# A decoder trunk on one core: GpSimd multiplies the keys by their decays, VectorE the queries, and 64 stationary keys for blocks of 64

## The chip, the cores and the metric

The kernel runs on one core of a Trainium2 chip. A core has TensorE (PE in the rows; PEld is its weight load), VectorE (DVE), ScalarE (ACT), GpSimd (POOL) and SyncE (SP), which here issues the loads. The metric is the time of one execution on the device in microseconds, the median of several runs.

## What is computed

A trunk of two pre-norm layers over 256 tokens of width 2048: the first mixes tokens with HGRN2 (12 heads of 128), the second with gated linear attention (GLA, 4 heads with keys of 192 and values of 384). Both share a projection with a cross attention into 256 memory tokens, and each layer ends with a SwiGLU feed-forward. All is float32. What matters here is the recurrence of both mixers, cut from the reference:

```python
def _chunk_gated_linear_attention(q, k, v, log_a):
    """S_t = diag(exp(log_a_t)) S_{t-1} + k_t v_t^T ; o_t = S_t^T q_t, causal."""
    ...
        diff = cum[:, :, :, None, :] - cum[:, :, None, :, :]
        decay = jnp.exp(jnp.where(mask[:, :, None], diff, -jnp.inf))
        scores = jnp.einsum('bhtd,bhsd,bhtsd->bhts', qc, kc, decay)
        intra = jnp.einsum('bhts,bhse->bhte', scores, vc)
```

A score of query t with key s thus carries, in each channel, the product of all decays between s and t.

## The kernel before

Every large matmul multiplies in two parts: a weight tile arrives by DMA as `raw` (four blocks of 128x512), ScalarE casts it to a rounded part, VectorE subtracts that from the raw tile to get the rest, both into a `parts` tile, and TensorE makes three products of them with the two parts of the activations. `project_two` goes over eight pairs of row blocks; a pair of kind S takes seven products instead of eight, for which VectorE first forms sums and differences of the raw blocks. At the end VectorE and ScalarE add the products up. So ScalarE, VectorE and TensorE work in a chain on tile after tile, and TensorE takes its instructions strictly in the program's order.

The scores stand between these projections. HGRN has three groups of four heads (`hgrn_group`), GLA two pairs of two heads (`gla_pair`). `gated_scores` makes the scores of all 256 tokens by doubling: queries `Q` and keys `K` lie with the 128 channels on the partitions. Level by level, for blocks of m = 1, 2, 4, ... 64 tokens, TensorE multiplies each second block of queries with the keys, 128 tokens at a time (`score`; `sdh`, `sph`, `slh` and `pxh` in HGRN, `sdg`, `spg`, `slg` and `pxg` in GLA are its banks). VectorE then copies what belongs to the level from the bank to the scores `sc` under a mask (`place`, the COPY_PREDICATED rows), and `grow(m)` multiplies the queries of the odd blocks by the decay of the block's first part and the keys of the even blocks by the decay of the second, so that both are right for the next level. The decay products `T` of all levels are made beforehand by `decays`. After level 64 `across` multiplies the second half's queries with all keys of the first (`pxh`, `pxg`). At a level m the stationary operand is the first `keys` tokens of 128; `keys` was `max(P - m, 96)`: 124, 120, 112, 96, 96 for blocks of 4 to 64.

Each level is a piece in a list (`later`). `project_two` calls `step()` at set places, and so puts a piece between its products. The tile framework then orders the instructions of each engine by its own plan and places the semaphores. `pe`, `ve` and `ac` are wrappers, which is why nearly all rows carry their one line, L141; instructions that are given to `nc.gpsimd` directly carry their own. GpSimd does little before: memsets, and the power -1/2 of each root mean square (`rstd`, L179).

Of the kernel before, what the change touches and what calls it, by code (L numbers as in the profile page):

```python
# [14 lines left out]
ALU = mybir.AluOpType  # L15
AX = mybir.AxisListType

P = 128
# [5 lines left out]
MIX = 1536  # L24
# [4 lines left out]
DK = 192  # L29
DV = 384  # L30
# [5 lines left out]
def trunk_kernel(ctx: ExitStack, tc: tile.TileContext, x, mem, norm_mix, norm_ffn, norm_mem,  # L36
                 norm_final, hgrn_w_in, hgrn_lb_logits, hgrn_onorm, gla_w_in, gla_w_gk,
                 gla_b_gk, gla_onorm, w_mem_kv, w_out, w_gate_up, w_down, c_ident, c_mask, out):
    nc = tc.nc
# [112 lines left out]
    pe, ve, ac = Engine(nc.tensor), Engine(nc.vector), Engine(nc.scalar)  # L152
# [83 lines left out]
    def later(*pieces):  # L236
        pending.extend(pieces)
# [13 lines left out]
    def side(shape, name):  # L251
        return wts.tile(shape, F32, tag="parts", name=name, bufs=6)
# [400 lines left out]
    def new_ss(name):  # L653
        return small.tile([P, NT, NQ], F32, tag="hss", name=name)
# [60 lines left out]
    for l in range(2):  # L715
        kv = side([P, 2, XH * T], f"kv{l}")
# [5 lines left out]
        if l == 0:  # L722
# [4 lines left out]
            hq, ss, first_turns = {}, new_ss("ss_x"), []  # L727
# [103 lines left out]
    def gated_scores(st, heads, name):  # L831

        nh = len(heads)
        ng = NT * nh

        def place(at, cols, i, ps, m):

            rows, n = ps.shape[0], at.shape[1]
            nb = 64 // m
            ve.copy_predicated(
                out=at[0:rows].rearrange("p g (b o m) -> p g b o m", o=2, m=m)[:, :, :, cols, :],
                mask=mask[0:rows, i, :].rearrange("p (b m) -> p b m", m=m).unsqueeze(1).broadcast_to([rows, n, nb, m]),
                data=ps.rearrange("p g (b m) -> p g b m", m=m))

        def grow(m):

            Q, K = st["Q"], st["K"]  # L850
            nb = K.shape[1] * T // (2 * m)
            tv = st["T"][m].rearrange("p (b o) -> p b o", o=2)
            qv = Q[:, 0, :, :].rearrange("p n (b o m) -> p (n b) o m", o=2, m=m)[:, :, 1 if m > 1 else 0, :]
            kv = K.rearrange("p n (b o m) -> p (n b) o m", o=2, m=m)[:, :, 0, :]
            ve.tensor_tensor(out=qv, in0=qv, in1=tv[:, :, 0].unsqueeze(2).broadcast_to([P, nb, m]), op=ALU.mult)
            ve.tensor_tensor(out=kv, in0=kv, in1=tv[:, :, 1].unsqueeze(2).broadcast_to([P, nb, m]), op=ALU.mult)

        def score(ps, f, t, q, i, parts, n=P):
            pe.matmul(ps[0:n], st["K"][:, f, t * P:t * P + n], q, start=i == 0, stop=i == len(parts) - 1)

        def even_diagonal():
            sc = st["sc"] = work.tile([P, ng, P], F32, tag="sc", name=f"sc{name}")
            nc.gpsimd.memset(sc, 0.0)
            ps = aux_ps(f"sd{name}").rearrange("p (g c) -> p g c", c=64)
            for t in range(NT):
                for a, parts in enumerate(heads):
                    for i, f in enumerate(parts):
                        q = st["Q"][:, 0, f, t * P:(t + 1) * P].rearrange("p (c o) -> p c o", o=2)[:, :, 0]
                        score(ps[:, t * nh + a, :], f, t, q, i, parts)
            place(sc, 0, 0, ps[:, 0:ng, :], 1)  # L870
            grow(1)

        def pairs():
            sc = st["sc"]
            for t in range(NT):
                ps = aux_ps(f"sp{name}{t}").rearrange("p (g x c) -> p g x c", x=2, c=64)
                for a, parts in enumerate(heads):
                    for i, f in enumerate(parts):
                        q = st["Q"][:, :, f, t * P:(t + 1) * P].rearrange("p x (b o m) -> p x b o m", o=2, m=2)[:, :, :, 1, :]
                        score(ps[:, a, :, :].rearrange("p x (b m) -> p x b m", m=2), f, t, q, i, parts)  # L880
                place(sc[:, t * nh:(t + 1) * nh, :], 1, 1, ps[:, 0:nh, 1, :], 1)
                place(sc[:, t * nh:(t + 1) * nh, :], 1, 2, ps[:, 0:nh, 0, :], 2)
            grow(2)

        def level(li):
            m = LEVELS[li]

            keys = max(P - m, 96)
            ps = aux_ps(f"sl{name}{m}").rearrange("p (g c) -> p g c", c=64)
            for t in range(NT):  # L890
                for a, parts in enumerate(heads):
                    for i, f in enumerate(parts):
                        q = st["Q"][:, 0, f, t * P:(t + 1) * P].rearrange("p (b o m) -> p b o m", o=2, m=m)[:, :, 1, :]
                        score(ps[:, t * nh + a, :].rearrange("p (b m) -> p b m", m=m), f, t, q, i, parts, keys)
            place(st["sc"], 1, 1 + li, ps[0:keys, 0:ng, :], m)
            grow(m)

        def across():
            scx = st["scx"] = work.tile([P, nh, P], F32, tag="scx", name=f"scx{name}")
            px = aux_ps(f"px{name}")  # L900
            for a, parts in enumerate(heads):
                for i, f in enumerate(parts):
                    score(px[:, a * P:(a + 1) * P], f, 0, st["Q"][:, 0, f, P:T], i, parts)
            ac.copy(out=scx.rearrange("p a t -> p (a t)"), in_=px[:, 0:nh * P])

        return [even_diagonal, None, pairs, None, lambda: level(2), lambda: level(3), None, lambda: level(4),
                lambda: level(5), None, lambda: level(6), across]

    def readout(st, a, nh, t, v, ops):
# [78 lines left out]
    def gla_pair(w, pr, dec, decay, hq, r, yq):  # L988

        kw = MIX // 2  # L990
# [15 lines left out]
        def read(a):  # L1006
            hd = 2 * pr + a
            for t in range(NT):
                po = aux_ps(f"gpo{hd}{t}")
                readout(st, a, 2, t, lambda s: v[a][:, s, :], po[:, 0:DV])  # L1010
                ss = small.tile([P, 4], F32, tag="oss", name=f"goss{hd}{t}")
                square_sum(po[:, 0:DV], ss[:, 0:1], f"go{hd}{t}")
                ro = rstd(ss[:, 0:1], 1, DV, f"gro{hd}{t}")
                ve.scalar_tensor_tensor(out=gate[a][:, t, :], in0=po[:, 0:DV], scalar=ro[:, 0:1],
                                               in1=gate[a][:, t, :], op0=ALU.mult, op1=ALU.mult)

        def turn_y(a):
            hd = 2 * pr + a
            for i in range(3):
                f = 3 * hd + i  # L1020
                q, k = divmod(f, 4)
                if k == 0:
                    yq[q] = Quad("tq", f"y1_{q}")
                tp = transposes([lambda t: gate[a][:, t, i * P:(i + 1) * P]], f"ty1_{f}")
                yq[q].put(k, 1, tp[:, 0:T], g_go[:, i:i + 1])
# [3 lines left out]
        def give():  # L1029
            for name in "kq":  # L1030
                dst.append(work.tile([P, NT, 2, T], F32, tag="stg", name=f"gs{name}{pr}", bufs=2))
                nc.gpsimd.memset(dst[-1][:, :, :, DK:T], 0.0)
            return [lambda t, d=d: d[:, t, :, 0:DK] for d in dst]

        project_two(hq["pairs"], "------S-", w, kw + pr * 2 * DK, pr * 2 * DK, 2 * DK, f"gk{pr}", give,
                    lambda ps: ps.rearrange("p (a c) -> p a c", c=DK))
        for d in dst:
            for t in range(NT):
# [3 lines left out]
        if pr == 0:  # L1042
            scores[5:5] = [lambda: decay(1), None]
        later(None, None, turn_k, turn_q, None, *scores)
        gate, v = [], []
        for a in range(2):
            def give():
                for dst, tag in ((gate, "gate"), (v, "v")):
                    dst.append(work.tile([P, NT, DV], F32, tag=tag, name=f"g{tag}{pr}{a}"))
                return [lambda t, d=d[a]: d[:, t, :] for d in (gate, v)]  # L1050

            project_two(hq["pairs"], "-----SS-" if a == 0 else "-----SS-", w, 2 * kw + MIX + (2 * pr + a) * DV, 2 * kw + (2 * pr + a) * DV, DV,
                        f"gg{pr}{a}", give)
            for dst, func in ((gate[a], AF.Silu), (v[a], AF.Copy)):
                for t in range(NT):
                    ac.activation(out=dst[:, t, :], in_=dst[:, t, :], func=func, scale=r[:, t:t + 1])
            later(None, None, lambda a=a: read(a), None, lambda a=a: turn_y(a))

    def gla(hq, r, yq):
# [47 lines left out]
        for pr in range(2):  # L1107
            gla_pair(w, pr, dec, decay, hq, r, yq)
# [114 lines left out]
    for l in range(2):  # L1223
# [33 lines left out]
        if l == 0:  # L1257
            hq = {}
# [81 lines left out]
```

## Time and profile before

| | us |
|---|---|
| median of three runs | 2284.35 (2283.91 to 2284.79) |
| the profiled execution | 2283.64 |
| its span in the trace | 2281.9 |
| TensorE busy | 2267.8 (99%) |
| VectorE busy | 2086.5 (91%) |
| ScalarE busy | 1404.9 (62%) |
| GpSimd busy | 35.3 (2%) |

The granted clock of TensorE was 2.4 GHz throughout (0.999 of it over the span). The scores take five stretches of the span: 180 to 255, 285 to 360 and 386 to 447 us in HGRN, 1297 to 1350 and 1416 to 1465 in GLA. A busy TensorE in the page is one that has matmuls in flight; how many it finishes is read from the starts of neighbouring rows. A row's duration includes a tail that overlaps the next instruction, so that what an instruction costs its engine is the distance to the next start.

### The profile page before, as it was taken

How to read it: one execution, taken by the hardware profiler on the slowest of the kernel's cores; microseconds unless marked ns; L12 is line 12 of the kernel's file. 1: busy time of each engine (PE TensorE's matmuls, PEld its weight loads, DVE VectorE, ACT ScalarE, POOL GpSimd, SP SyncE). 2: the span in 40 equal slices, each digit the busy share in tenths (PEclk: the TensorE clock that was granted, in tenths of full speed). 3: DMA queues.
4: the chain of work that ended last, by engine and by line, in shares of the span. 5: the costliest groups of instructions: out<-in, count | busy, mean ns of one | idle time of the engine just before them, and what ended most of it. 6: DMA issues, size and time to landing. Idle time of an engine off the chain costs nothing.

```text
span 2281.9 us, 29717 instructions
## 1 busy us (share of the span) xinstructions
PE 2267.8 (99%) x10942; PEld 1922.5 (84%) x10942; DVE 2086.5 (91%) x2605; ACT 1404.9 (62%) x1918; POOL 35.3 (2%) x39
## 2 busy tenths in 40 slices
PE   9999999999999999999999999999999999999998
PEld 7888888888888888888889999988888888888887
DVE  7889999799999999999997887889999999999997
ACT  7655546466666666666665665466566666666664
POOL 0000000000000000000000000001000000000000
PEclk9999999999999999999999999999999999999999
DMA  8545545545556655565565446455565566556664
GB/s 292 198 161 167 185 148 184 166 150 202 184 203 206 213 191 202 200 206 203 201 209 179 140 143 190 144 184 203 180 208 203 203 200 206 203 201 205 204 210 158
DMA packets 231650, 435.57 MB, mean 191 GB/s; under 512 B 12204, under 2 KB 41680, under 8 KB 231248
## 3 DMA queue, kind: packets, MB, share of 16 engines
q1 hardware_dynamic: 230208, 429.41, 55.9%
q10 hardware_dynamic: 1296, 4.26, 0.5%
q8 instruction: 86, 1.41, 0.2%
q14 instruction: 60, 0.49, 0.1%
HBM read 430.48 MB, written 3.15 MB: 190 GB/s over the span
## 4 chain that ended last, share of the span: by engine, by line
PE 86%; issue 9%; DVE 3%; ACT 1%; DMA 0%; POOL 0%; SPq 0%; POOLq 0%; DVEq 0%; ACTq 0%
PE f_p L141 36%; PE fd L141 19%; PE wo L141 4%; PE hv2p L141 2%; PE m1p L141 2%; PE wo0p L141 2%; PE wo1p L141 2%; PE fd_0p L141 2%; PE m0p L141 2%; PE gk1p L141 1%; PE gg10p L141 1%; PE gg11p L141 1%; PE gg01p L141 1%; PE gx L141 1%; DVE raw L141 1%
## 5 line engine op out<-in xcount | busy, mean ns | idle before, releaser
L141 DVE TENSOR_TENSOR raw<-raw 128x512 f32<-128x512 f32 (+3 forms) x474 | 403.0, 851 | 9.4
L141 DVE TENSOR_TENSOR parts<-raw,parts 128x1024 fp32r<-128x1024 f32 (+1 forms) x216 | 246.3, 1179 | 15.5 <-ACT parts L141 15.5
L141 ACT CAST parts<-raw 128x1024 fp32r<-128x1024 f32 (+1 forms) x216 | 211.7, 1017 | 45.1 <-DMA raw<-in_w_out_dram 9.1
L141 ACT COPY h<-fd 128x512 f32<-128x512 f32 x80 | 46.0, 588 | 51.9 <-PE fd L141 49.2
L141 ACT ACTIVATE s<-s,rf_r 128x512 f32<-128x512 f32 x44 | 31.9, 725 | 44.5 <-DVE s L141 44.5
L141 DVE TENSOR_TENSOR e<-f_p,e 128x512 f32<-128x512 f32 x66 | 45.1, 684 | 2.7 <-DVE s L141 0.5
L141 ACT COPY fd<-h 128x512 f32<-128x512 f32 x82 | 45.2, 583 | 0.0
L141 PE MATMUL fd<-parts,s_2h 128*128 128x512 f32 x128 | 39.8, 392 | 0.0
L141 PE MATMUL fd<-parts,s_8h 128*128 128x512 f32 x128 | 39.8, 392 | 0.0
L141 PE MATMUL fd<-parts,s_4h 128*128 128x512 f32 x128 | 39.8, 392 | 0.0
L141 PE MATMUL fd<-parts,s_0h 128*128 128x512 f32 x128 | 39.8, 392 | 0.0
L141 PE MATMUL fd<-parts,s_6h 128*128 128x512 f32 x128 | 39.8, 392 | 0.0
L141 PE MATMUL fd<-parts,s_1h 128*128 128x512 f32 x128 | 39.4, 389 | 0.0
L141 PE MATMUL fd<-parts,s_7h 128*128 128x512 f32 x128 | 39.4, 389 | 0.0
L141 PE MATMUL fd<-parts,s_3h 128*128 128x512 f32 x128 | 39.4, 389 | 0.0
L141 PE MATMUL fd<-parts,s_5h 128*128 128x512 f32 x128 | 39.4, 389 | 0.0
L141 DVE TENSOR_TENSOR s<-f_p,e 128x512 f32<-128x512 f32 x44 | 30.3, 688 | 4.6 <-PE f_p L141 2.8
L141 DVE SCALAR_TENSOR_TENSOR s<-e,rf_r,s 128x512 f32<-128x512 f32 x44 | 31.0, 745 | 0.2
L141 PEld LDWEIGHTS fd<-parts,s_3h 128*128 128x128 f32 x128 | 24.0, 188 | 5.0
L141 PEld LDWEIGHTS fd<-parts,s_1h 128*128 128x128 f32 x128 | 24.0, 188 | 5.0
L141 PEld LDWEIGHTS fd<-parts,s_7h 128*128 128x128 f32 x128 | 24.0, 188 | 5.0
L141 PEld LDWEIGHTS fd<-parts,s_5h 128*128 128x128 f32 x128 | 24.0, 188 | 5.0
(5696 smaller groups left out, 7231.6 us busy)
## 6 DMA issues: line engine op xcount, KB each, us to landing
raw<-in_w_gate_up_dram SPq DMA_DIRECT2D x352, 512.0 KB, 4.1
raw<-in_w_down_dram SPq DMA_DIRECT2D x80, 1024.0 KB, 5.1
raw<-in_hgrn_w_in_dram SPq DMA_DIRECT2D x96, 512.0 KB, 4.0
raw<-in_gla_w_in_dram SPq DMA_DIRECT2D x96, 384.0 KB, 3.5
raw<-in_w_out_dram SPq DMA_DIRECT2D x16, 1024.0 KB, 5.0
raw<-in_w_out_dram SPq DMA_DIRECT2D x32, 512.0 KB, 4.2
raw<-in_w_mem_kv_dram SPq DMA_DIRECT2D x30, 512.0 KB, 5.4
raw<-in_w_down_dram SPq DMA_DIRECT2D x16, 512.0 KB, 4.7
```

Of the source, the lines that this page charges most:

```text
L141: ins = func(*args, **kwargs)
```

## The change

In `grow` the multiply of the keys goes to GpSimd and is no longer behind the multiply of the queries on VectorE. For blocks of 64 the stationary operand is 64 keys instead of 96, and `place` copies 64 rows. The other lines of the diff only write the plans of the GLA projections as tables and leave them as they were.

```diff
             ve.tensor_tensor(out=qv, in0=qv, in1=tv[:, :, 0].unsqueeze(2).broadcast_to([P, nb, m]), op=ALU.mult)
-            ve.tensor_tensor(out=kv, in0=kv, in1=tv[:, :, 1].unsqueeze(2).broadcast_to([P, nb, m]), op=ALU.mult)
+            nc.gpsimd.tensor_tensor(out=kv, in0=kv, in1=tv[:, :, 1].unsqueeze(2).broadcast_to([P, nb, m]), op=ALU.mult)
...
-            keys = max(P - m, 96)
+            keys = P - m if m == 64 else max(P - m, 96)
```

The framework's plan changes with it. GpSimd's order, the first HGRN group (`K_1569` its keys, `F` and `Th` its decays, `sch` the scores, `ro_r` the powers of the readout), the difference with + for the rows that are new:

```order
 L863 MEMSET sch_1644 128x1024
+L856 TENSOR_TENSOR K_1569<-K_1569,F_1568 128x512
+L856 TENSOR_TENSOR K_1569<-K_1569,Th_1585 128x256x2
+L856 TENSOR_TENSOR K_1569<-K_1569,Th_1585 128x128x4
+L856 TENSOR_TENSOR K_1569<-K_1569,Th_1585 128x64x8
+L856 TENSOR_TENSOR K_1569<-K_1569,Th_1585 128x32x16
+L856 TENSOR_TENSOR K_1569<-K_1569,Th_1585 128x16x32
+L856 TENSOR_TENSOR K_1569<-K_1569,Th_1585 128x8x64
 L179 TENSOR_TENSOR ro_r<-ro_v,mhalf 128x4
```

The seven multiplies of the group stand between the clearing of its scores and the power of its readout. Each waits for the score matmuls that read the old keys, for its decays and for the multiply before it.

VectorE's order in the same group, from the copy of level 16 (`slh_1954`) to that of level 64 (`slh_2027`), before:

```order
L141 COPY_PREDICATED sch_1644<-mask,slh_1954 112x32x16
L141 TENSOR_TENSOR Q_1598<-Q_1598,Th_1585 128x32x16
L141 TENSOR_TENSOR K_1569<-K_1569,Th_1585 128x32x16
L141 TENSOR_TENSOR parts37a<-raw_2006,parts37a 128x1024
L141 TENSOR_TENSOR parts37b<-raw_2006,parts37b 128x1024
L141 COPY_PREDICATED sch_1644<-mask,slh_1982 96x16x32
L141 TENSOR_TENSOR Q_1598<-Q_1598,Th_1585 128x16x32
L141 TENSOR_TENSOR K_1569<-K_1569,Th_1585 128x16x32
L141 TENSOR_TENSOR parts38a<-raw_2051,parts38a 128x1024
L141 TENSOR_TENSOR parts38b<-raw_2051,parts38b 128x1024
L141 TENSOR_TENSOR parts39a<-raw_2091,parts39a 128x1024
L141 COPY_PREDICATED sch_1644<-mask,slh_2027 96x8x64
```

And now, from the two additions from PSUM (`hv0p`) ahead of the copy of level 16:

```order
L141 TENSOR_TENSOR gates_1895<-hv0p_1564,gates_1895 128x512
L141 TENSOR_TENSOR gates_1895<-hv0p_1560,gates_1895 128x512
L141 COPY_PREDICATED sch_1644<-mask,slh_1954 112x32x16
L141 TENSOR_TENSOR Q_1598<-Q_1598,Th_1585 128x32x16
L141 TENSOR_TENSOR parts38a<-raw_2051,parts38a 128x1024
L141 TENSOR_TENSOR parts38b<-raw_2051,parts38b 128x1024
L141 COPY_PREDICATED sch_1644<-mask,slh_1982 96x16x32
L141 TENSOR_TENSOR Q_1598<-Q_1598,Th_1585 128x16x32
L141 TENSOR_TENSOR parts39a<-raw_2091,parts39a 128x1024
L141 TENSOR_TENSOR parts40a<-raw_2172,parts40a 128x512
L141 TENSOR_TENSOR raw_2172<-raw_2172 128x1024
L141 TENSOR_TENSOR parts39b<-raw_2091,parts39b 128x1024
```

The key multiplies are gone from VectorE, and the splits of the weight tiles have moved about one tile ahead of the copies: tiles 37 stood behind the copy of level 16 and now stand before it; behind the copy of level 32 there is one tile more than before.

TensorE's order in the same group, at the scores of level 32 (`slh_1982`; `hf1p` are the products of the next projection):

```order
 L141 MATMUL hf1p_1978<-parts36a,hx3x 128x512 x3
+L141 MATMUL slh_1982<-Q_1598,K_1569 96x64 x8
 L141 MATMUL hf1p_1966<-parts36b,hx3x 128x512 x3
-L141 MATMUL hf1p_1970<-parts36b,hx3x 128x512
-L141 MATMUL slh_1982<-Q_1598,K_1569 96x64 x8
-L141 MATMUL hf1p_1970<-parts36b,hx3x 128x512 x2
+L141 MATMUL hf1p_1970<-parts36b,hx3x 128x512 x3
```

The scores of level 32 stand four matmuls earlier, directly behind those of parts36a. Each of the eight score matmuls of an order's row is two records in the trace.

TensorE's order in the second GLA pair, from the scores of level 64 (`slg_12067`) to the last ones (`pxg_12101`; `gg11p` are the products of a projection):

```order
-L141 MATMUL slg_12067<-GQ_11677,GK_11658 96x64 x8
+L141 MATMUL slg_12067<-GQ_11677,GK_11658 64x64 x8
 L141 MATMUL gg11p_12051<-parts264b,hm_2x 128x384 x3
 L141 MATMUL gg11p_12055<-parts264b,hm_2x 128x384 x3
 L141 MATMUL gg11p_12059<-parts264b,hm_2x 128x384 x3
 L141 MATMUL gg11p_12063<-parts264b,hm_2x 128x384 x3
+L141 MATMUL pxg_12101<-GQ_11677,GK_11658 128x128 x4
 L141 MATMUL gg11p_12051<-parts265a,hm_3x 128x384 x3
-L141 MATMUL gg11p_12055<-parts265a,hm_3x 128x384
-L141 MATMUL pxg_12101<-GQ_11677,GK_11658 128x128 x4
```

The last scores stand four matmuls earlier too, 12 matmuls behind those of level 64.

## Rows read from the trace of the kernel before

**Rows 1.** busy time of each engine, and the chain by engine; the page

```profile
PE 2267.8 (99%) x10942; PEld 1922.5 (84%) x10942; DVE 2086.5 (91%) x2605; ACT 1404.9 (62%) x1918; POOL 35.3 (2%) x39
...
PE 86%; issue 9%; DVE 3%; ACT 1%; DMA 0%; POOL 0%; SPq 0%; POOLq 0%; DVEq 0%; ACTq 0%
```

**Rows 2.** windows: us, then busy us (instructions) of each engine, clock, DMA share, GB/s

```profile
180.00:255.00 75.00, 74.97 (x415) 64.07 (x414) 69.64 (x90) 37.78 (x55) 0.00 (x0) 1.00 0.47 150
...
1416.00:1465.00 49.00, 49.00 (x335) 48.98 (x334) 40.25 (x63) 21.49 (x35) 0.00 (x0) 1.00 0.46 145
```

**Rows 3.** tile K of HGRN: ns min/median/max, first and last start, form

```profile
L141 DVE TENSOR_TENSOR K<-K,Th x18: 675/682/733, 198.7 to 443.3; 128x512 f32<-128x512 f32 x18
```

**Rows 4.** tile GK of GLA, the same columns

```profile
L141 DVE TENSOR_TENSOR GK<-GK,Tg x12: 679/683/718, 1308.4 to 1460.2; 128x512 f32<-128x512 f32 x12
```

**Rows 5.** timeline of TensorE, first HGRN group: start us, us, what

```profile
216.15 0.61 PE L141 MATMUL hv0p<-parts34c,hx2m 128*128 128x512 f32 x2
...
218.62 0.85 PE L141 MATMUL hv0p<-parts34b,hx2x 128*128 128x512 f32 x3
219.30 0.84 PE L141 MATMUL hv0p<-parts34d,hx2x 128*128 128x512 f32 x3
...
227.81 1.69 PE L141 MATMUL slh<-Q,K 128*112 128x64 f32 x16
229.31 3.00 PE L141 MATMUL hf1p<-parts36a,hx3x 128*128 128x512 f32 x12
...
233.06 1.49 PE L141 MATMUL slh<-Q,K 128*96 128x64 f32 x16
234.36 2.09 PE L141 MATMUL hf1p<-parts36b,hx3x 128*128 128x512 f32 x8
...
239.02 1.49 PE L141 MATMUL slh<-Q,K 128*96 128x64 f32 x16
```

**Rows 6.** timeline of VectorE, first HGRN group

```profile
216.77 1.23 DVE L141 TENSOR_TENSOR parts34d<-raw,parts34d 128x1024 fp32r<-128x1024 f32 x1 [1.20 <-ACT parts34d L141]
...
240.55 0.74 DVE L141 COPY_PREDICATED sch<-mask,slh 96x512 f32<-96x512 uint8 x1 [0.66 <-PE slh L141]
...
241.78 0.68 DVE L141 TENSOR_TENSOR K<-K,Th 128x512 f32<-128x512 f32 x1
```

**Rows 7.** timeline of GpSimd, whole span

```profile
40.85 0.67 POOL L116 CAST mask<-maskf 128x512 uint8<-128x512 f32 x1 [7.80 <-DMA maskf<-in_mask_dram]
...
451.46 1.01 POOL L179 TENSOR_TENSOR ro_r<-ro_v,mhalf 128x4 f32<-128x4 f32 x1 [90.12 <-DVE ro_v L141]
...
1356.25 0.55 POOL L179 TENSOR_TENSOR gro_r<-gro_v,mhalf 128x1 f32<-128x1 f32 x1 [32.38 <-DVE gro_v L141]
...
1588.23 9.30 POOL L179 TENSOR_TENSOR rf_r<-rf_v,mhalf 128x2 f32<-128x2 f32 x1 [83.03 <-DVE rf_v L141]
```

**Rows 8.** window of the longest GpSimd instruction, VectorE alone

```profile
1588.23:1597.53 9.30, 9.30 (x16) 1.00 0.65 226
```

**Rows 9.** timeline of VectorE beside GpSimd's cast

```profile
40.97 0.87 DVE L141 SCALAR_TENSOR_TENSOR mem3l<-tp_mem3h,gm,mem3h 128x256 fp32r<-128x256 f32 x2
41.75 0.68 DVE L141 TENSOR_TENSOR raw<-raw 128x512 f32<-128x512 f32 x1
```

**Rows 10.** timeline of TensorE, GLA

```profile
1337.63 1.49 PE L141 MATMUL slg<-GQ,GK 128*96 128x64 f32 x16
...
1435.35 0.68 PE L141 MATMUL gg10p<-parts260a,hm_6x 128*128 128x384 f32 x3
...
1459.01 2.33 PE L141 MATMUL gg11p<-parts264b,hm_2x 128*128 128x384 f32 x12
```

**Rows 11.** timeline of VectorE, GLA

```profile
1335.74 0.43 DVE L141 COPY_PREDICATED scg<-mask,slg 112x256 f32<-112x256 uint8 x1
...
1433.49 0.43 DVE L141 COPY_PREDICATED scg<-mask,slg 124x256 f32<-124x256 uint8 x1
...
1459.24 0.44 DVE L141 COPY_PREDICATED scg<-mask,slg 96x256 f32<-96x256 uint8 x1 [0.34 <-PE slg L141]
```

More of the change, by code (lines that the diff above doesn't have):

```diff
@@ L1033, in give @@
             return [lambda t, d=d: d[:, t, :, 0:DK] for d in dst]
-        project_two(hq["pairs"], "------S-", w, kw + pr * 2 * DK, pr * 2 * DK, 2 * DK, f"gk{pr}", give,
+        project_two(hq["pairs"], ("------S-", "------S-")[pr], w, kw + pr * 2 * DK, pr * 2 * DK, 2 * DK, f"gk{pr}", give,
                     lambda ps: ps.rearrange("p (a c) -> p a c", c=DK))
@@ L1044, in gla_pair @@
         later(None, None, turn_k, turn_q, None, *scores)
+        GLA = (("-----SS-", "-----SS-"), ("-----SS-", "-----SS-"))
         gate, v = [], []
@@ L1050, in give @@
                 return [lambda t, d=d[a]: d[:, t, :] for d in (gate, v)]
-            project_two(hq["pairs"], "-----SS-" if a == 0 else "-----SS-", w, 2 * kw + MIX + (2 * pr + a) * DV, 2 * kw + (2 * pr + a) * DV, DV,
+            project_two(hq["pairs"], GLA[pr][a], w, 2 * kw + MIX + (2 * pr + a) * DV, 2 * kw + (2 * pr + a) * DV, DV,
                         f"gg{pr}{a}", give)
```

## The prediction, made before the changed kernel ran

> **What bounds the kernel now.** The first part of the page and the chain of work come first [rows 1]: TensorE is busy 2267.8 of 2281.9 us and holds 86% of the chain, while VectorE is busy 91% and stands on 3% of it. GpSimd has 35.3 us in all. The windows of the scores follow [rows 2]: in the first HGRN group TensorE is busy 74.97 of 75 us and VectorE 69.64; in the second GLA pair TensorE is busy all 49 us and VectorE 40.25. So TensorE bounds the stretches that the change touches. Work taken from VectorE is worth something only where TensorE waits for a result of VectorE, and a wait that is put in front of a score matmul is lost for good, since TensorE has no idle time to give back. The rest of the working therefore asks, level by level, when the keys and queries are ready and when TensorE wants them.
>
> **Part 1: 64 stationary keys.** A level's scores are 16 matmul records. With 112 keys they take 1.50 us (227.81 to 229.31), with 96 keys 1.30 us (233.06 to 234.36) [rows 5], that is 93.8 and 81.3 ns for one, 0.78 ns a key. Carried on to 64 keys this is 56 ns, 0.90 us for the level: 0.40 us less. The trace has no level under 96 keys, so the saving lies between 0 (the 64 columns that stream through may set a floor) and 0.40. I take 0.40, because the row nearest below still lies on the line. Five scores (three HGRN groups, two GLA pairs) make 2.0 us, all on TensorE. The masked copy after it covers 64 rows instead of 96, and its time goes by its columns (0.74 us, [rows 6]): nothing.
>
> **Part 2: VectorE without the key multiplies.** Seven levels in five scores are 35 multiplies of 128x512. One lasts 682 ns [rows 3, 4], and the next instruction starts 0.60 us after it (240.55, 241.78 and the query multiply between, [rows 6]): 21 us of VectorE's time. Under a TensorE that is never idle they are worth nothing by themselves. One place is on the path: in the first group TensorE takes 2.47 us for the nine matmuls from 216.15 to 218.62, where the three from 218.62 take 0.68 [rows 5]; nine at 0.227 would be 2.04, so 0.43 us are lost to the late parts34d, whose subtraction VectorE starts at 216.77 after 1.20 us of waiting for ScalarE [rows 6], itself behind VectorE's work on raw. Three key multiplies lie ahead of it, 1.8 us, and the new order does the raw tile earlier. The second group has the same rows. Value: 0.9 us, between 0 and 0.9.
>
> **Part 3: the multiply on GpSimd.** Its duration is in no row. GpSimd's cast of 128x512, one operand, took 0.67 us [rows 7]: the lower bound. Two operands read one after the other would be twice that, 1.34, which I take as the nearest. The other far end is the power, the only two-operand arithmetic that GpSimd does here: 0.55 us for one element and 1.01 for four [rows 7], 0.16 us an element, which would be 80 us for 512. I leave that end out, because a power is many steps and a multiply is one; but it says that the duration may be well over 1.34, and the third case below prices 2.5. The Trainium skill's "GPSIMD Engine Reference" (section on elementwise cycle accounting) gives 4497 ns for a two-input add of 2048 elements and calls GpSimd the wrong engine for it; scaled, that is an estimate of 1.12 us, and with it the stalls below would be 0.5 us instead of 0.8.
>
> When does it start? It waits for the scores that read the old keys, not for VectorE's copy or query multiply, since the decays are long done. Then it needs SBUF. The power at 1588.23 lasted 9.30 us instead of 0.55 [rows 7], and in those 9.30 us VectorE ran 16 instructions without a break [rows 8], all with two SBUF operands; so a stream of these keeps GpSimd out. The cast at 40.85 ran its 0.67 us while VectorE did two operations with one operand in PSUM (40.97, 0.87 us) and had ended before the next two-SBUF operation at 41.75 [rows 7, 9]; so PSUM work lets it in. Each level's masked copy has its data in PSUM and runs just when the multiply becomes ready. I assume that GpSimd gets in there at the latest and, as the unfavourable end, that VectorE's query multiply then waits until it is through. No row shows that second half. The Trainium skill's "SBUF — State Buffer" (section "Who interferes with whom") says it: a VectorE instruction with two SBUF inputs and a GpSimd one that reads SBUF exclude each other for a whole instruction. By that the sum stands as it is; without it the 0.8 would be about 0.2.
>
> Now the slack. Between the ends of one level's scores and the start of the next TensorE has 12 matmuls at the tightest: 2.7 us in HGRN, where the changed order puts level 32 directly behind parts36a, and 2.1 in GLA. The multiply, then the blocked query multiply, need 1.34 + 0.68 = 2.0 us plus whatever time the port was busy first.
> HGRN, level 16 to 32: scores end at 229.31; VectorE then adds from PSUM, so 229.4 + 1.34 = 230.7; the queries follow by 231.9; TensorE wants them at 232.0. No stall. Level 64 to the last scores: VectorE's splits, of which three now stand ahead of the copy, end about 239.9 (an estimate from their spacings of 1.13 and 0.60 us), the multiply at 241.2, queries 241.9; wanted at 242.3. No stall.
> GLA pair 0, level 16 to 32: the split before the copy ends at 1335.74 [rows 11]; multiply to 1337.08, queries to 1337.76; wanted at 1337.63 [rows 10]: 0.1.
> GLA pair 1, level 4 to 8: copy at 1433.49 [rows 11], queries 1435.5; wanted at 1435.35, since the changed order drops the three matmuls that stood ahead [rows 10]: 0.2. Level 64 to the last scores: they end at 1459.01 - 0.40 = 1458.6, the split now ahead of the copy keeps the port to about 1459.3 (before, the copy began at 1459.24), multiply 1460.6, queries 1461.3; wanted 2.1 us after 1458.6, about 1460.75 [rows 10, 11]: 0.5. Other levels have 3 us and more.
> Stalls: 0.8 us, between 0 and the rivals' prices. GpSimd's own queue behind a waiting multiply holds only a readout's power, a memset of the next scores and, in GLA, two memsets whose inputs are there in time: nothing.
>
> **The sum.** -2.0 - 0.9 + 0.8 = -2.1 us on TensorE's path. The profiled execution took 2283.64 us, 1.74 above its span of 2281.9, and 0.7 below the median of 2284.35. It becomes 2281.5; the median becomes **2282.2**, 0.09% less.
>
> **Rivals.**
> 1. GpSimd doesn't get in under the masked copy, or only partly, and stays out until VectorE runs dry. For: the 9.30 us, and VectorE's 93% in the window. Against: the cast at 40.85. Place: levels 32 and 64 of each HGRN group, where splits follow the query multiply. VectorE would work on until its next copy, which waits for scores that wait for the keys: about 239.9 + 1.34 against a wanted 238.7, 2.5 us; about as much, to 3.5, at the last scores. Six us in three groups are 18, GLA about 3 (its four adds from PSUM follow the queries). 21 - 2.9 = +18: 2302, slower. It decides as soon as the port stays closed past one query multiply.
> 2. The multiply is longer than its slack. From 2.0 to 2.1 us on, each further microsecond falls on two places in each HGRN group and on five in the GLA pairs. At 2.5 us HGRN loses some 3.5 us and GLA 6: +9.5 - 2.9 = +6.6, 2291, slower.
> 3. VectorE's relief reaches further than the one place, and nothing stalls: -2.0 and -0.9 are 2281.4, and another 1.7 us would have to come from waits that I don't see (the windows leave 0.03 us of idle TensorE in 75, [rows 2]). Faster by over 0.2% only then.
> 4. The change doesn't do what it says: VectorE waits for GpSimd as long as it multiplied before, 64 columns cost as 96 did: 2284, no change.
>
> **How the numbers follow.** What a measurement of this kernel can tell from no change is about 0.2%, 4.6 us: 2279.8 to 2288.9 counts as the same. Forecast 0.56, with its own range from 2280.3 (no stall) to 2285 (no saving on keys and parts34d, stalls of 0.8). Rival 1 0.12, rival 2 0.13, rival 3 0.09, of which 0.08 below 2279.8, rival 4 0.10. So the same 0.67, slower 0.25, faster 0.08. The range runs from 2279.5 to 2294: it takes in rival 2 at 2.5 us and the lighter part of rival 1, and leaves out the full rival 1 (0.10) and some 0.06 below.
>
> **What would show it.** Scores of 64 keys at 0.9 us for 16 records: part 1. TensorE's nine matmuls of parts34 in 2.04 us: part 2. GpSimd's 35 multiplies at about 1.3 us each by their spacing, starting within 0.2 us of the masked copy, and query multiplies that start late by what is left of them: part 3. TensorE idle ahead of slh 64 and pxh in HGRN with GpSimd as the releaser: rival 1; ahead of slg 32 and pxg in GLA with multiplies above 2.1 us: rival 2. The prediction is wrong if a GpSimd multiply lasts over 2.2 us or if VectorE's two-SBUF stream keeps it out for longer than one level's slack.

## The result, and the profile of the changed kernel

The changed kernel takes 2292.60 us, the median of six runs (2290.13 to 2295.14), against 2284.13 for the kernel before on the same chip (six runs, 2283.31 to 2284.79). The ratio is 1.0037, with a 95% interval from 1.0027 to 1.0047: slower by 0.37%, about 8.5 us. The prediction said 2282.2 and no change. The profiled execution took 2291.03 us.

Busy time of each engine and the chain by engine, from the page of after (before: [rows 1]):

```profile
PE 2269.7 (99%) x10942; PEld 1920.7 (84%) x10942; DVE 2084.1 (91%) x2570; ACT 1406.5 (61%) x1918; POOL 96.9 (4%) x74
...
PE 76%; DVE 2%; ACT 1%; issue 1%; DMA 0%; POOL 0%; SPq 0%; POOLq 0%; DVEq 0%; ACTq 0%
```

The shares look almost as before. GpSimd has 61.6 us more, about 1.8 us for each of 35 instructions; VectorE, rid of 35 multiplies, is busy for only 2.4 us less. Both say that the two engines waited inside their instructions. What TensorE waited for in after (engine, line, releaser: us in all, times, the longest):

```profile
PE slh L141 <- POOL K L856: 4.3, 3, 1.8
PE slg L141 <- POOL GK L856: 1.6, 1, 1.6
...
PE pxg L141 <- POOL GK L856: 0.6, 1, 0.6
...
PE slg L141 <- DVE GQ L141: 0.5, 1, 0.5
...
PE pxg L141 <- DVE GQ L141: 0.2, 1, 0.2
```

These seven waits, 7.2 us, the kernel before did not have. The three of HGRN and the long one of GLA are at the same place each time: the scores of level 32 wait for the keys that the multiply of level 16 makes. The multiplies on GpSimd in after (ns min/median/max, first and last start, form; before: [rows 3, 4]):

```profile
L856 POOL TENSOR_TENSOR K<-K,Th x18: 1104/1414/4457, 195.8 to 446.2; 128x512 f32<-128x512 f32 x18
L856 POOL TENSOR_TENSOR GK<-GK,Tg x12: 1109/1753/3583, 1310.3 to 1466.0; 128x512 f32<-128x512 f32 x12
```

The same 512 elements take from 1.10 to 4.46 us. The first HGRN group from the scores of level 16 on, TensorE in after (start, us, what, idle before it and its releaser; before: [rows 5]):

```profile
226.90 1.69 PE L141 MATMUL slh<-Q,K 128*112 128x64 f32 x16
228.40 3.00 PE L141 MATMUL hf1p<-parts36a,hx3x 128*128 128x512 f32 x12
233.24 2.15 PE L141 MATMUL slh<-Q,K 128*96 128x64 f32 x16 [1.83 <-POOL K L856]
235.14 4.07 PE L141 MATMUL hf1p<-parts36b,hx3x 128*128 128x512 f32 x12
239.05 1.29 PE L141 MATMUL hf1p<-parts37a,hx4x 128*128 128x512 f32 x5
```

VectorE there:

```profile
228.68 0.72 DVE L141 COPY_PREDICATED sch<-mask,slh 112x512 f32<-112x512 uint8 x1
229.29 0.68 DVE L141 TENSOR_TENSOR Q<-Q,Th 128x512 f32<-128x512 f32 x1
229.89 1.22 DVE L141 TENSOR_TENSOR parts38a<-raw,parts38a 128x1024 fp32r<-128x1024 f32 x1
231.02 1.22 DVE L141 TENSOR_TENSOR parts38b<-raw,parts38b 128x1024 fp32r<-128x1024 f32 x1
235.42 0.72 DVE L141 COPY_PREDICATED sch<-mask,slh 96x512 f32<-96x512 uint8 x1 [3.18 <-PE slh L141]
236.04 1.53 DVE L141 TENSOR_TENSOR Q<-Q,Th 128x512 f32<-128x512 f32 x1
```

And GpSimd:

```profile
228.73 4.45 POOL L856 TENSOR_TENSOR K<-K,Th 128x512 f32<-128x512 f32 x1 [5.93 <-PE slh L141]
235.52 1.51 POOL L856 TENSOR_TENSOR K<-K,Th 128x512 f32<-128x512 f32 x1 [2.34 <-PE slh L141]
```

At level 16 GpSimd's multiply begins at 228.73, inside the copy. VectorE goes from the copy to the query multiply and to two splits, all at their usual times (0.68, 1.22, 1.22), and has nothing more to do at about 232.15. Only 1.03 us after that GpSimd is through, at 233.18, and TensorE, whose 12 matmuls of parts36a ended at 231.40, goes on at 233.24. At level 32 it is the other way: the multiply begins at 235.52, ends at 237.03, which is 0.99 us after the copy's end at 236.04, so it got in there; VectorE's query multiply, which begins at 236.04, takes 1.53 instead of 0.68 us.

After the stall TensorE is slow. Windows of that stretch in after (us, then busy us of each engine, granted clock, DMA share, GB/s):

```profile
228.00:233.30 5.30, 3.47 (x20) 2.62 (x18) 4.25 (x6) 3.10 (x5) 4.45 (x1) 1.00 0.64 199
233.30:240.00 6.70, 6.70 (x33) 5.76 (x34) 4.54 (x5) 0.70 (x1) 1.51 (x1) 0.75 0.49 158
240.00:250.00 10.00, 10.00 (x60) 8.29 (x59) 9.06 (x10) 3.54 (x6) 1.50 (x1) 1.00 0.33 105
```

The granted clock is 0.75 over 6.7 us: half of that time at 1.2 instead of 2.4 GHz, or 1.7 us lost, and the 12 matmuls of parts36b take 3.91 us to the next start instead of 2.84. In the second group TensorE idles as long and the clock stays; the same 16 records take 1.38 us to the next start there, against 1.90 in the first group:

```profile
337.76 1.57 PE L141 MATMUL slh<-Q,K 128*96 128x64 f32 x16 [1.84 <-POOL K L856]
339.14 3.00 PE L141 MATMUL hf2p<-parts52b,hx3x 128*128 128x512 f32 x12
```

So the 7.3 us by which the span grew (2281.9 to 2289.2) are: +7.2 of waits; +1.7 because each of the seven costs about 0.24 more than its idle (the 3.00 of parts36a has a tail of 0.16, and the next 16 records take 0.08 more when nothing is in flight); +1.6 of clock; -0.8 for parts34 and 50, as predicted; -1.2 for parts42 and 58, not predicted; -0.6 for the 64 keys. That is 7.9; the two executions differ by half a microsecond before the first score.

### The profile page after: what moved, and what is told of

Same layout as the page of the kernel before. It is cut to its first block, busy times and chain, and to the rows that moved or that the text cites. A ratio compares the mean times of both kernels' runs of the same rounds, so it can differ in the third digit from the quotient of the medians.

```text
span 2289.2 us, 29762 instructions
## 1 busy us (share of the span) xinstructions
PE 2269.7 (99%) x10942; PEld 1920.7 (84%) x10942; DVE 2084.1 (91%) x2570; ACT 1406.5 (61%) x1918; POOL 96.9 (4%) x74
## 4 chain that ended last, share of the span: by engine, by line
PE 76%; DVE 2%; ACT 1%; issue 1%; DMA 0%; POOL 0%; SPq 0%; POOLq 0%; DVEq 0%; ACTq 0%
PE f_p L141 37%; PE fd L141 18%; PE wo L141 4%; PE wo0p L141 2%; PE wo1p L141 2%; PE fd_0p L141 2%; PE gk1p L141 1%; PE gg10p L141 1%; PE gg11p L141 1%; PE gg01p L141 1%; PE gx L141 1%; PE gk0p L141 1%; DVE raw L141 1%; PE gg00p L141 1%; PE slg L141 0%
## 5 line engine op out<-in xcount | busy, mean ns | idle before, releaser
L856 POOL TENSOR_TENSOR K<-K,Th 128x512 f32<-128x512 f32 x18 | 32.0, 1779 | 125.3 <-PE slh L141 77.1
L141 PEld LDWEIGHTS slh<-Q,K 128*124 128x124 f32 (+4 forms) x240 | 24.2, 174 | 7.4 <-POOL K L856 5.6
```

The lines of the kernel that those rows point to most:

```text
L141: ins = func(*args, **kwargs)
L856: nc.gpsimd.tensor_tensor(out=kv, in0=kv, in1=tv[:, :, 1].unsqueeze(2).broadcast_to([P, nb, m]), op=ALU.mult)
```

## Experiments

The theory after this reading, A: GpSimd needs 1.1 us and has its slack, but where VectorE's next instruction is a ready one with two SBUF operands it is passed over, one after the other, until VectorE comes to something else or runs dry; this happens at level 16. It does not say why at level 32 above, where the query multiply stood ready too, GpSimd came first; the last experiment asks about that. Rivals: B, the framework's new order of splits and scores costs, not the engine; C, GpSimd is too slow at every level; D, it is the block shape of level 16. Each kernel is compared with runs of the kernel before that were taken with it on the same chip.

**The 64 keys alone (e_keys).** No GpSimd; every engine's order is that of before.

```diff
-            keys = max(P - m, 96)
+            keys = P - m if m == 64 else max(P - m, 96)
```

> The kernel before with 64 stationary keys for blocks of 64 alone; the order on every engine is that of before. In the trace of after the 16 records of that score took 1.08 us to the next start, against 1.30 with 96 keys: 0.22 us in each of five scores is 1.1 us, so 2283.0 against 2284.1. The straight line of the prediction (0.40 each) would give 2282.1. If the width does nothing for the time, 2284.1.

Measured: 2282.38 us (11 runs, 2281.70 to 2283.49) against 2283.18 (27 runs): 0.80 less, ratio 0.9997 (0.9988 to 1.0005), so that the median alone does not show a gain. TensorE in the first group, before and then in this kernel:

```profile
236.29 2.89 PE L141 MATMUL hf1p<-parts37a,hx4x 128*128 128x512 f32 x12
...
240.32 2.99 PE L141 MATMUL hf1p<-parts37b,hx4x 128*128 128x512 f32 x12
```

```profile
235.72 2.89 PE L141 MATMUL hf1p<-parts37a,hx4x 128*128 128x512 f32 x12
238.54 1.15 PE L141 MATMUL slh<-Q,K 128*64 128x64 f32 x16
239.62 3.02 PE L141 MATMUL hf1p<-parts37b,hx4x 128*128 128x512 f32 x12
```

The score takes 1.08 us to the next start, 0.22 less than with 96 keys [rows 5]; but the matmuls ahead of it take 2.82 instead of 2.73, so that from parts37a to parts37b 3.90 us pass instead of 4.03. In all five scores 0.11 to 0.13 us is left, 0.6 together; that is what reaches the time.

**The multiply alone (e_mult).** After with 96 keys; every engine's order is that of after.

```diff
-            keys = P - m if m == 64 else max(P - m, 96)
+            keys = max(P - m, 96)
```

> The multiply on GpSimd alone, 96 keys at level 64; the order on every engine is that of after. All theories that blame the multiply or the new order say that it carries the loss: 2292.6 + 1.1 = 2293.7, between 2292.5 and 2295. If the loss came from the 64 keys it would be back at 2284.

Measured: 2292.70 us (5 runs, 2290.62 to 2294.39), ratio 1.0042 (1.0029 to 1.0054). The multiply on GpSimd, with the order that comes with it, carries the whole loss.

**Level 16 back on VectorE (e_not16).**

```diff
-            nc.gpsimd.tensor_tensor(out=kv, ...)
+            (ve if m == 16 else nc.gpsimd).tensor_tensor(out=kv, ...)
```

> As after, but the multiply for blocks of 16 is back on VectorE; the orders are those of after but for a few rows. Theory A (GpSimd is shut out by the stream of VectorE's instructions at this level): the stalls ahead of the scores of level 32 go (4.3 us in HGRN, 1.6 and 0.5 in GLA), and with them the lower clock after them; what is left are 0.8 us ahead of the last GLA scores: 2283 to 2285. Theory B (the framework's new order costs, not the engine): 2291 or more. Theory C (GpSimd's multiply is too slow at every level): only its share goes, 2288 to 2290.

Measured: 2281.79 us (11 runs, 2280.90 to 2282.46), ratio 0.9993 (0.9985 to 1.0002). That is below the 2283 to 2285 that I expected, mostly because before itself took 0.9 us less here than in the runs that I had reckoned from. Five of 35 multiplies carry the whole loss; of the waits the 0.8 us ahead of the last GLA scores are left, as expected. B and C fall: the order is that of after but for a few rows, and 30 multiplies remain on GpSimd.

**The queries ahead of the copy (e_swap).** VectorE's order is that of after but for this one exchange; the other engines' is unchanged.

```diff
-            place(st["sc"], 1, 1 + li, ps[0:keys, 0:ng, :], m)
             grow(m)
+            place(st["sc"], 1, 1 + li, ps[0:keys, 0:ng, :], m)
```

> As after, but from blocks of 4 on VectorE multiplies the queries ahead of the masked copy; nothing else moves. Theory A, in the form that GpSimd gets in where VectorE passes from a two-SBUF instruction to the copy, but is often passed over where VectorE passes from the copy to the query multiply: each key multiply ends about 0.6 + 1.1 = 1.7 us after its scores, no query multiply waits, no stall is left: 2282 to 2283. Theory B: unchanged, 2291 to 2293. Theory C (a multiply that is too slow by itself, or a port that stays shut under the copy as well): stalls stay, 2288 or more.

Measured: 2281.51 us (11 runs, 2280.82 to 2281.98), 1.67 below before's median, ratio 0.9993 (0.9984 to 1.0002); I had expected 2282 to 2283. VectorE at level 16:

```profile
229.41 0.68 DVE L141 TENSOR_TENSOR Q<-Q,Th 128x512 f32<-128x512 f32 x1
230.01 0.72 DVE L141 COPY_PREDICATED sch<-mask,slh 112x512 f32<-112x512 uint8 x1
230.62 1.50 DVE L141 TENSOR_TENSOR parts38a<-raw,parts38a 128x1024 fp32r<-128x1024 f32 x1
```

GpSimd, and TensorE:

```profile
229.46 1.57 POOL L856 TENSOR_TENSOR K<-K,Th 128x512 f32<-128x512 f32 x1 [5.92 <-PE slh L141]
```

```profile
229.13 3.00 PE L141 MATMUL hf1p<-parts36a,hx3x 128*128 128x512 f32 x12
231.97 1.49 PE L141 MATMUL slh<-Q,K 128*96 128x64 f32 x16
```

The multiply is through at 231.03, 1.02 us after the query multiply ended and the copy began, so it got in there. The copy runs beside it in its usual time, and the split behind the copy waits 0.3 us, which nobody misses. The longest multiply of HGRN lasts 1.62 us, and TensorE waits for none; 0.4 us ahead of two GLA scores are left, for queries.

**The queries wait for the keys, at level 16 alone (e_hold).** The order of every engine is that of after; the query multiply of that level waits for GpSimd's semaphore.

```diff
+            if m == 16:
+                tc.add_manual_dep(qin.ins, kin.ins.name, ... Sync ...)
```

> As after, with one wait more in each score: for blocks of 16 the query multiply on VectorE waits for the key multiply on GpSimd. The order is that of after. Theory A (what costs is that VectorE's query multiply and the splits behind it pass the waiting GpSimd): the multiply now gets in when the copy of level 16 ends, is through about 1.0 us later instead of 3 to 4, the queries 0.6 after it: no stall ahead of level 32, which needs less than the 2.7 us (HGRN) and 2.1 us (GLA) of slack; left are 0.8 us ahead of the last GLA scores: 2281.5 to 2283. If the added wait costs as much as being passed over (VectorE stands still 1.0 us a level), 2288 or more.

Measured: 2282.12 us (11 runs, 2281.11 to 2283.27), ratio 0.9993 (0.9984 to 1.0002). VectorE and GpSimd at level 16 of the first group:

```profile
229.12 0.73 DVE L141 COPY_PREDICATED sch<-mask,slh 112x512 f32<-112x512 uint8 x1
230.29 0.69 DVE L141 TENSOR_TENSOR Q<-Q,Th 128x512 f32<-128x512 f32 x1 [0.43 <-POOL K L855]
```

```profile
229.17 1.08 POOL L855 TENSOR_TENSOR K<-K,Th 128x512 f32<-128x512 f32 x1 [5.93 <-PE slh L141]
```

The sharpest of the runs. The multiply begins 0.05 us into the same copy as in after, and takes 1.08 us instead of 4.45. All five multiplies of that level take 1.08, which in after took 4.45, 4.46, 3.26, 1.75 and 3.58. My expectation said that the copy would keep it out until its end: it does not. What kept it out in after was the ready query multiply behind the copy. One added wait in each score, 0.43 us of VectorE's time in the first group, saves about 10 us. With the order of after on every engine, it also rules out B by itself.

**Level 16 alone on GpSimd, in nearly the order of before (e_only16).**

```diff
-            ve.tensor_tensor(out=kv, ...)
+            (nc.gpsimd if m == 16 else ve).tensor_tensor(out=kv, ...)
```

> The kernel before with the multiply for blocks of 16 alone on GpSimd, 96 keys kept. In HGRN a split (36b, 52b) still stands on VectorE between the end of the level's scores and the copy, as before. Theory A, with the rule that GpSimd gets in where a split ends and the copy begins: the multiply ends 1.0 us after the copy's start, the queries 0.55 later, no stall in HGRN: 2282.5 to 2284. Rival D (at this level VectorE's stream shuts GpSimd out whatever stands ahead of the copy, because of the block shape): the multiply would end about 1 us after split 37b, some 1 to 2 us too late in each of three groups, more in GLA: 2287 to 2291.

Measured: 2285.91 us (11 runs, 2284.47 to 2286.67) against 2283.74: 2.2 more, ratio 1.0008 (0.9999 to 1.0017). VectorE in the first group, and GpSimd in the first group, the third, and the second GLA pair:

```profile
228.47 1.22 DVE L141 TENSOR_TENSOR parts36b<-raw,parts36b 128x1024 fp32r<-128x1024 f32 x1
229.60 0.74 DVE L141 COPY_PREDICATED sch<-mask,slh 112x512 f32<-112x512 uint8 x1
230.23 0.94 DVE L141 TENSOR_TENSOR Q<-Q,Th 128x512 f32<-128x512 f32 x1
```

```profile
228.84 1.79 POOL L856 TENSOR_TENSOR K<-K,Th 128x512 f32<-128x512 f32 x1 [74.02 <-PE slh L141]
...
427.03 3.26 POOL L856 TENSOR_TENSOR K<-K,Th 128x512 f32<-128x512 f32 x1 [67.14 <-PE slh L141]
...
1449.82 3.60 POOL L856 TENSOR_TENSOR GK<-GK,Tg 128x512 f32<-128x512 f32 x1 [65.82 <-PE slg L141]
```

My number missed by 2 us, since I had looked at the first two groups only. There a split is under way when the keys are free; the multiply waits for its end, gets in as the copy begins at 229.60, and is through 1.03 us later, at 230.63. In the third group and in the second GLA pair VectorE is idle ahead of the copy, the multiply begins 0.10 us into the copy, and it is passed over as in after (waits of 0.6 and 1.6 us ahead of the next scores). The two waits alone make the 2.2; in the profiled run the clock fell as well after the second, and what made up for that is not worked out. The same block shape goes both ways: D falls. What decides here is what VectorE does when the multiply becomes ready.

**The exchange without GpSimd (e_vswap).** Before with 64 keys and the exchange of e_swap, the key multiplies on VectorE; the order is otherwise nearly that of before.

> No GpSimd: the kernel before with 64 keys and the query multiply ahead of the masked copy from blocks of 4 on, the keys on VectorE. If the swap by itself were worth the gain of e_swap over before, 2281.5; if that gain needs the multiply off VectorE, as e_keys: 2282.4, at most 0.5 less.

Measured: 2283.11 us (11 runs, 2281.80 to 2283.97) against 2283.74: 0.63 less, ratio 0.9996 (0.9988 to 1.0005). That is e_keys again. The further 0.9 us of e_swap do not come from the exchange by itself; they come with the multiply off VectorE and the order that the framework then makes, which no run separates, and both intervals hold 1.

**The rows of the copy (e_rows16, e_rows112).** At level 32 of HGRN GpSimd comes first at the copy's end, at level 16 last. Their copies have 96 and 112 rows.

```diff
-            keys = P - m if m == 64 else max(P - m, 96)
+            keys = P - m if m == 64 else 96 if m == 16 else max(P - m, 96)    # e_rows16
...
+            keys = max(P - m, 112)                                            # e_rows112
```

> As after, with 96 instead of 112 stationary keys and copied rows for blocks of 16 (scores of 16 keys are left out there), to see what decides at the end of the copy: with 96 rows GpSimd gets in ahead of the query multiply in level 32 of HGRN. If the rows decide, the multiplies of level 16 last 1.5 us and the stalls ahead of level 32 go in HGRN; if the block shape or something else decides, 4.4 us as in after.

> As after, with 112 stationary keys and copied rows for blocks of 32 and 64 too (the rows added are masked out). It asks whether the number of rows in the copy decides who comes first at its end. In HGRN, GpSimd came first with 96 and 64 rows in all multiplies that became ready inside such a copy, and last with 112 rows. If the rows decide, the multiplies of levels 32 and 64 in HGRN that begin inside the copy are now passed over too and last 2.5 us and more, with stalls ahead of the scores of level 64 and of the last ones, 2295 or more. If they don't, these multiplies last 1.5 us as in after and the time is that of after plus 2 to 3 us of wider scores, about 2294 with the stalls at the places of after.

The edits change the stationary keys and the copied rows together, so the rows stand here for both. The kernel of e_rows16 leaves out the scores of 16 keys of 112 at level 16; it is there for its trace alone.

Measured, one run each: 2282.91 with 96 rows at level 16, and 2311.51 with 112 rows at all three levels, 28.2 above before. VectorE and GpSimd of e_rows16 in the third group, where the multiply again begins 0.10 us into the copy (in the first two it began 0.15 us ahead of it):

```profile
425.02 0.72 DVE L141 COPY_PREDICATED sch<-mask,slh 96x512 f32<-96x512 uint8 x1 [1.69 <-PE slh L141]
425.64 1.56 DVE L141 TENSOR_TENSOR Q<-Q,Th 128x512 f32<-128x512 f32 x1
```

```profile
425.12 1.54 POOL L856 TENSOR_TENSOR K<-K,Th 128x512 f32<-128x512 f32 x1 [5.74 <-PE slh L141]
```

GpSimd of e_rows112 at levels 32 and 64 of the first group, then TensorE at the last scores and a window around them:

```profile
236.53 3.85 POOL L856 TENSOR_TENSOR K<-K,Th 128x512 f32<-128x512 f32 x1 [3.07 <-PE slh L141]
245.72 6.73 POOL L856 TENSOR_TENSOR K<-K,Th 128x512 f32<-128x512 f32 x1 [5.34 <-issue]
```

```profile
252.50 1.86 PE L141 MATMUL pxh<-Q,K 128*128 128x128 f32 x7 [4.11 <-POOL K L856]
```

```profile
225.00:260.00 35.00, 29.06 (x133) 24.26 (x132) 19.93 (x23) 11.29 (x14) 15.03 (x3) 0.80 0.29 97
```

With 112 rows the multiplies of levels 32 and 64, which took 1.1 to 1.5 us in after, are now passed over too, in all three groups (3.85, 6.73; 3.86, 6.72; 2.12, 3.25 us). TensorE waits 15.4 us for GpSimd, and the granted clock, 0.994 over the span against 0.999 before, takes some 11 more. In HGRN, then, the rows decide at levels 16, 32 and 64 who comes first at the copy's end. It is no rule for other levels: at level 8, with 120 rows and a query multiply ready behind the copy, GpSimd is not kept out at all. VectorE and GpSimd there, third group of after:

```profile
424.67 0.71 DVE L141 COPY_PREDICATED sch<-mask,slh 120x512 f32<-120x512 uint8 x1
425.28 1.14 DVE L141 TENSOR_TENSOR Q<-Q,Th 128x512 f32<-128x512 f32 x1
```

```profile
424.77 1.10 POOL L856 TENSOR_TENSOR K<-K,Th 128x512 f32<-128x512 f32 x1 [12.82 <-PE slh L141]
```

## Why the prediction was wrong

**What bounds the kernel** held: TensorE has no idle time to give back, and every wait put in front of a score was lost, with 0.24 us and sometimes 1.7 us of clock on top.

**Part 1** was mis-sized. The score of 64 keys takes 1.08 us, not 0.90, and about 0.6 us of the 2.0 reached the time (e_keys). The line through 112 and 96 keys does not go on to 64.

**Part 2** was right in its place and too small. The nine matmuls of parts34 take 2.04 us in after (215.68 to 217.72), 0.43 less. But the same late splits of the sum and difference blocks stood in the waits of before further down, and I did not look for them:

```profile
PE hf1p L141 <- DVE parts42d L141: 0.3, 1, 0.3
PE hf2p L141 <- DVE parts58d L141: 0.3, 1, 0.3
```

Both are gone in after, and the matmuls there start 0.6 us earlier each time. The relief is 2.0 us, not 0.9; that is the third rival's mechanism, with two more places.

**Part 3 is where it failed.** The duration was not the fault: 1.08 to 1.11 us for blocks of 8 and more when VectorE leaves it alone, between the lower bound of 0.67 and the 1.34 that I took. The Trainium skill's "GPSIMD Engine Reference" (elementwise cycle accounting), from which the prediction had an estimate of 1.12, agrees with that. Two side sums were wrong: by the prediction's own rows a multiply of 1.12 us makes the stalls 0.3, not 0.5, and query multiplies that do not wait make them nothing, not 0.2; neither is in the forecast. The failed step is the sentence that GpSimd gets in under the masked copy at the latest and that VectorE's query multiply then waits. I had put the start of level 16's multiply 0.1 us after the next matmul's start (229.4 against 229.31), under VectorE's additions from PSUM. In after it begins 0.33 us after it (228.73 against 228.40), and by then the additions are through and the copy has begun; the query multiply is ready behind the copy, and VectorE passes GpSimd with that and with both splits. So the slack of 2.7 us, which would have done for 1.1 + 0.7, met 4.45. In GLA the assumed sequence did happen once: at level 16 of the first pair GpSimd waits for a split, gets in as the copy begins, and the query multiply is held up (1.24 us); the wait there is 0.5 us where I had put 0.1. The 0.2 in the second pair did not come. At its last scores, where I had put 0.5, it is 0.6, but because the multiply is passed over (2.68 us).

The Trainium skill's "SBUF — State Buffer" (section "Who interferes with whom") has it that whoever issues first gets the shared ports for a whole instruction. The trace agrees at level 32 (GpSimd's multiply began 0.52 us before the query multiply, which was held up, 1.53 us). It does not agree at level 16: GpSimd's multiply began 0.56 us before the query multiply and was passed by three instructions. There the measurement decides: a start that the trace shows for GpSimd does not mean that it is served.

e_hold is the kernel of my sentence: it forces VectorE's query multiply to wait at that level, and takes 2282.12 us. The prediction was 2282.2. The closeness owes something to luck, since the 64 keys gave 1.4 us less and the relief 1.1 more than I had put; but the sum failed on who comes first, not on a duration. That 2292.60 lies inside my range is luck too: the range reached to 2294 for multiplies that are long by themselves and for a lighter first rival at other levels.

**The rivals.** The first, that VectorE's stream shuts GpSimd out until it runs dry, was the mechanism, at 12%. I had it at levels 32 and 64, with 21 us; it came at level 16, where the new order had put two ready splits behind the query multiply, with 7 us of waits. The 9.30 us of a power beside 16 two-operand instructions [rows 7, 8] had shown it; I gave more weight to a cast beside two PSUM operations [rows 9], which was no contest: the next instruction with two SBUF operands came at 41.75, after the cast had ended. In e_rows112 the rival came true at its own places, 2311.5 where I had put 2302. The second rival fell: no multiply is over 1.6 us long by itself.

**The clock** was in no term. The kernel before hardly lets TensorE idle in these stretches [rows 2], so its trace did not show the price.

What is left open: why the rows decide in HGRN (112 rows: passed over in all nine multiplies of levels 16 to 64 in e_rows112, which began inside a copy; 96 and 64 rows: first in all those of the other kernels that did), while in GLA, where the copy is shorter (0.44 us), GpSimd is passed over with 112, 96 and 64 rows alike; and why at level 8 it goes through at once inside a copy of 120 rows, in HGRN (1.10 us) and in the second GLA pair (1.11 us from 1442.30). That a ready query multiply and ready splits behind the copy keep GpSimd out is shown by e_hold; when they do and when they don't is not.

## What to carry to other kernels

Between GpSimd and VectorE a multiply's duration is the smaller question; ask what VectorE has ready at the moment GpSimd's instruction becomes ready, and how many two-SBUF instructions stand behind it, since that is how long the stall can get. Put a copy that reads PSUM, or one wait, behind the point where GpSimd must come in: here the exchange of two lines (e_swap) turns +8.5 us into -1.7 against before, every one of its 11 runs (2281.98 at most) below every one of before's 27 (2282.42 at least), though the interval of the ratio still holds 1. And where TensorE has no idle time, price a stall at more than its length.

## What the runs showed of the hardware

GpSimd's multiply of 128x512 with a broadcast operand takes 1.06 to 1.12 us for blocks of 8 and more where VectorE does not hold it up, 1.16 for blocks of 4, 1.32 for 2 and 1.53 for single elements. A masked copy from PSUM runs beside it at its usual time (e_hold, e_swap).

TensorE's clock fell after four of the seven waits over 1.6 us in the traces of after, e_mult and e_only16, to 1.2 GHz, at 1.7 us of lost time each, and stayed at 2.4 GHz after the other three and after all shorter ones there. The length of the wait does not decide it: in after it fell after 1.83 us and not after 1.84. This may be why the runs of after and e_mult spread over 5.0 and 3.8 us and those of e_swap over 1.2; that is not shown run by run.
